# Pacing one stream of weight loads through a feed-forward stage, splitting GpSimd's subtractions, and leaving out eight dot products

## The chip, the cores and the metric

The kernel runs on one core of one Trainium2 chip. The metric is the time of one execution on the device, in microseconds (us). Five engines take part, each with its own queue of instructions that it works off in order: TensorE (PE in the profile; its weight loads are PEld), VectorE (DVE), ScalarE (ACT), GpSimd (POOL) and SyncE (SP), which here issues the transfers from and to the main memory (DMAs).

## The reference

The reference runs two blocks over a sequence of 512 tokens of width 1024. Cut to what matters:

```python
def first_block(x, ...):
    x = x + 0.5 * swiglu(rms_norm(x, ffn1_norm), ffn1_w_in, ffn1_w_out)   # the first FFN, D_FF = 2816
    ...                                # RWKV-7 time mixing, dilated attention, gates, w_out
    x = x + 0.5 * swiglu(rms_norm(x, ffn2_norm), ffn2_w_in, ffn2_w_out)   # the second FFN

def hybrid_layer(x, ctx, c, c_ctx, row, col, last, ...):                  # twice
    shift, scale, gate = split(silu(c) @ w_mod + b_mod, 3)                # the modulation
    shift_c, scale_c, gate_c = split(silu(c_ctx) @ w_mod + b_mod, 3)
    h  = rms_norm(x, norm_w) * (1 + scale) + shift
    hc = rms_norm(ctx, norm_w) * (1 + scale_c) + shift_c
    ...                                # latent attention, grouped attention, convolution
    x_new = x + gate * (y @ w_out)
    if last:
        return x_new, ctx
    ctx_new = ctx + gate_c * (yc @ w_out)
    return x_new, ctx_new
```

All values are 32-bit floats. The modulation is, for each of the two layers, 24 groups of 128 outputs (8 of shift, 8 of scale, 8 of gate), each for two vectors of length 1024: c and c_ctx. In the last layer gate_c is computed from its definition but used by nobody, since ctx is returned as it is.

## The kernel before

**Products in three parts.** Each weight chunk comes from the main memory as a tile wraw of 128 x up to 1024 floats (wload, L570, 512 KB for 1024 columns, two buffers). ScalarE rounds it into whi, the form that TensorE takes (L583), and the rest, wraw - whi, goes into wlo (L585 to L587). The argument on says who subtracts: 0 is GpSimd in one instruction, a number above 0 is VectorE in so many instructions. whi and wlo have three buffers each. The inputs stand in pairs in the same way (HH and HL, FH and FL), and each product is three matmuls: whi by high, whi by low, wlo by high (mm3, L617). A chunk of 1024 columns is eight slices of 128 columns, and so 24 matmuls of 128x128 by 128x512; wlo is first read by the third. wfill (L591) keeps one chunk split and one more loaded ahead of the chunk in use.

**The first FFN** (ffn_steps and ffn_stream, L701 to L813) has 44 chunks of w1 (22 pairs: gate, pg, and up, pu) and 24 of w2 (po), in the order 16 of w1, 8 of w2, 14, 8, 14, 8: 68 chunks in all, those of w2 with 8, 7 and 7 slices. After each pair of w1 chunks the gating runs (act, L731): on VectorE fa = pg x rs, then after ScalarE's tanh fa = (fs + 1) x fa, fb = pu x rs, fb = fb x fa, then after ScalarE's rounding FH, FL = fb - FH. Two of these five read the accumulators (PSUM) and rs; three have both operands in SBUF. Four accumulators (ffmm) are free for pg, pu and po. All of these chunks are split with on = 0, by GpSimd. The low-rank projections (pl, lora_steps) follow the FFN.

**The modulation** (mod_steps, L1531) is computed during the first FFN: 48 tiles wm of 128 x 1024 floats are loaded through SP (L1544, two buffers), and for each VectorE makes two dot products with the broadcast vectors (L1547, scalar_tensor_tensor with an accumulated sum, into the throw-away tile mjunk), one for c and one for c_ctx. The results M are next read in the second FFN.

**What sets the order.** The kernel's steps are generators. drive (L438) runs them twice: first it records an order by its own clock of the engines (Clock, L192, with costs such as 130 + 2.13 n ns for a GpSimd instruction with n columns), taking the step that could start first; a step's priority is added to that time, and mod_steps has 2000 ns. A step may wait for a flag (flags, need, count, L421 and L650 to L666). The second run replays the order. Below it a scheduler orders the instructions of each engine by a priority that counts up with each instruction; FF1_LATE (L21) puts mod_steps 500 back. Each engine then works off its queue in that order, and waits for semaphores only at its head.

Line 318, which every row of the profile names, is the helper through which all instructions go; rows are told apart by tile.

Of the kernel before, what the change touches and what calls it, by code (L numbers as in the profile page):

```python
# [17 lines left out]
RW_PRIO = {"stream": 2000, "fill": 5000}  # L18
RW_LATE = {"rw_stream": 500, "rw_fill": 500, "qkv_chain": -1000}
RW_AHEAD = 3000  # L20
FF1_LATE = {"norm": -500, "stats": -300, "mod_steps": 500}  # L21
FF2_PRIO = 300
X_LATE = {"proj_steps": 1000, "taps": 1000, "out_steps": 300}
# [168 lines left out]
class Clock:  # L192
    def __init__(self):
        self.t = {e: 0.0 for e in ("PE", "DVE", "ACT", "POOL", "SP")}
        self.gaps = {e: [] for e in self.t}
        self.room = GAPS[0]
        self.dma = 0.0
        self.acc = {}
        self.floor = {}
        self.slots = {}  # L200
        self.act_set = None
        self.last = 0.0
        self.free_run = False
# [324 lines left out]
class K:  # L528
    def __init__(self, tc, A, ctx, plan):
        self.clk = Clock()  # L530
        self.plan = plan
        self.flags = Flags(self.clk)
        self.A = A
        self.tc = _TC(tc, self.clk)
        self.nc = nc = _NC(tc.nc, self.clk)
        tc = self.tc
        E = ctx.enter_context
        self.const = E(tc.tile_pool(name="const", bufs=1))
        self.xp = E(tc.tile_pool(name="xp", bufs=1))
        self.hp = E(tc.tile_pool(name="hp", bufs=1))  # L540
        self.wp = E(tc.tile_pool(name="wp", bufs=3))
        self.sm = E(tc.tile_pool(name="sm", bufs=2))
        self.wraw, self.wq, self.wi = [], [], 0
        self.held = False
        self.fine = 4
        self.late = {}
        self.tk, self.nb = {}, {}
        npar = A["par"].shape[1]
        self.onescol = self.const.tile([P, 1], F32, name="onescol")
        nc.vector.memset(self.onescol, 1.0)  # L550

        warm = self.sm.tile([P, 1], F32, name="warm", bufs=1)
        nc.scalar.activation(warm, self.onescol, AF.Silu)
        self.wfill(0, 1)
        self.par_t = self.cload("par", [P, npar])
        self.acc = self.const.tile([P, T], F32, name="acc")
        self.M = [self.const.tile([P, 24, 2], F32, name=f"mod{l}") for l in range(2)]
# [12 lines left out]
    def wload(self, name, idx, a, b):  # L570
        raw = self.wp.tile([P, 1024], F32, tag="wraw", name="wraw", bufs=2)
        src = self.A[name]
        for i in idx:
            src = src[i] if not isinstance(i, tuple) else src[:, i[0]:i[1]]
        self.nc.sync.dma_start(raw[:, :a * b].rearrange("p (a b) -> p a b", a=a), src)
        return raw, a, b

    def wsplit(self, raw, a, b, on):
        nc = self.nc
        n = a * b  # L580
        hi = self.wp.tile([P, 1024], F32R, tag="whi", name="whi", bufs=3)
        lo = self.wp.tile([P, 1024], F32R, tag="wlo", name="wlo", bufs=3)
        nc.scalar.copy(hi[:, :n], raw[:, :n])  # L583

        for i in range(max(on, 1)):  # L585
            s = slice(i * n // max(on, 1), (i + 1) * n // max(on, 1))
            (nc.vector if on else nc.gpsimd).tensor_sub(lo[:, s], raw[:, s], hi[:, s].bitcast(F32))  # L587
        v = lambda t: t[:, :n].rearrange("p (a b) -> p a b", a=a)
        return v(hi), v(lo)
# [624 lines left out]
    def rw_tile(self, H, w, fin=None, chain=None):  # L1214
# [5 lines left out]
        for x in range(8):  # L1220

            ahead = RW_AHEAD if x % 4 else 0
            self.tc._tc.cur_priority -= ahead
# [307 lines left out]
    def mod_steps(self, stack):  # L1531

        nc = self.nc
        mp = stack.enter_context(self.tc.tile_pool(name="modp", bufs=1))
        cc = mp.tile([P, 2, 1024], F32, name="cc")
        junk = mp.tile([P, 1024], F32, name="mjunk")
        yield "Fffn1_normrs", 1, "ACT"
        nc.sync.dma_start(cc, self.A["cc"])
        nc.scalar.activation(cc, cc, AF.Silu)
        for l in range(2):  # L1540
            M = self.M[l]
            for m in range(24):
                w = mp.tile([P, 1024], F32, tag="wm", name="wm", bufs=2)
                nc.sync.dma_start(w, self.A[f"l_mod_{l}"][m])  # L1544
                for s in range(2):
                    yield "DVE"
                    nc.vector.scalar_tensor_tensor(junk, w, 1.0, cc[:, s], ALU.mult, ALU.mult, accum_out=M[:, m, s:s + 1])  # L1547
            yield "DVE"
            o, n = PAR_COLS[f"b_mod_{l}"]
            nc.vector.tensor_add(M, M, self.par_t[:, o:o + 24].unsqueeze(2).to_broadcast([P, 24, 2]))  # L1550
            o, n = PAR_COLS[f"norm_w_{l}"]
            nc.vector.tensor_scalar_add(M[:, 8:16], M[:, 8:16], 1.0)
            nc.vector.tensor_mul(M[:, 8:16], M[:, 8:16], self.par_t[:, o:o + 8].unsqueeze(2).to_broadcast([P, 8, 2]))

            nc.vector.tensor_scalar_mul(M[:, 16:24], M[:, 16:24], 0.5)
# [875 lines left out]
def body(tc, A, out, plan):  # L2431
    with ExitStack() as ctx:
# [9 lines left out]
        with ExitStack() as lor:  # L2442
            k.lora_setup(lor)
            k.late = FF1_LATE
            with ExitStack() as c2:
# [51 lines left out]
```

## Time and profile before

| | us |
|---|---|
| median of three runs | 2564.78 |
| lowest and highest of the three | 2545.41 and 2572.88 |
| the profiled execution | 2555.58 |
| its span, first to last instruction | 2553.8 |

The mean granted TensorE clock of the profiled execution is 0.948 of full speed. The page of the profile gives the busy time of each engine and the chain of work that ended last, followed back from the last instruction; further views are the table of busy times by stage, the timeline of an engine, the waits and the groups of equal instructions. A row of a timeline has the start, the duration, the engine, the operation and the tiles (out<-in); what stands in brackets is the idle time before it and what ended that.

### The profile page before, as it was taken

How to read it: one execution, taken by the hardware profiler on the slowest of the kernel's cores; microseconds unless marked ns; L12 is line 12 of the kernel's file. 1: busy time of each engine (PE TensorE's matmuls, PEld its weight loads, DVE VectorE, ACT ScalarE, POOL GpSimd, SP SyncE). 2: the span in 40 equal slices, each digit the busy share in tenths (PEclk: the TensorE clock that was granted, in tenths of full speed). 3: DMA queues.
4: the chain of work that ended last, by engine and by line, in shares of the span. 5: the costliest groups of instructions: out<-in, count | busy, mean ns of one | idle time of the engine just before them, and what ended most of it. 6: DMA issues, size and time to landing. Idle time of an engine off the chain costs nothing.

```text
span 2553.8 us, 33817 instructions
## 1 busy us (share of the span) xinstructions
PE 2372.9 (93%) x12556; PEld 1920.0 (75%) x12556; DVE 1703.2 (67%) x3157; ACT 1014.7 (40%) x1852; POOL 745.1 (29%) x441
## 2 busy tenths in 40 slices
PE   8798999999999999989989899999889999789897
PEld 6576887877777777757878788888677778677776
DVE  8999357676666656534767846664559865568865
ACT  4212224334233333335433533333335655345553
POOL 4444443010111110212423233335332332232331
PEclk9998999999889869979999999999899999899998
DMA  6555323433223224332423232433310222310221
GB/s 210 188 199 180 100 95 107 121 86 102 79 56 105 66 56 117 130 121 79 127 96 113 82 128 74 145 109 112 128 61 25 71 63 67 116 47 26 64 78 53
DMA packets 122196, 254.24 MB, mean 100 GB/s; under 512 B 39208, under 2 KB 54576, under 8 KB 121392
## 3 DMA queue, kind: packets, MB, share of 16 engines
q1 hardware_dynamic: 122032, 252.09, 31.6%
q8 instruction: 99, 1.62, 0.3%
q14 instruction: 65, 0.53, 0.1%
HBM read 222.07 MB, written 21.59 MB: 95 GB/s over the span
## 4 chain that ended last, share of the span: by engine, by line
PE 68%; DVE 19%; ACT 4%; issue 4%; DMA 2%; POOL 2%; SPq 0%; DVEq 0%; ACTq 0%; POOLq 0%
PE prj L318 12%; PE po L318 11%; PE pj L318 7%; PE pu L318 6%; PE pg L318 6%; DVE mjunk L318 5%; PE pm L318 4%; PE pwo L318 4%; PE sc L318 3%; PE pt L318 2%; DVE c0cy L318 1%; DVE fb L318 1%; PE pA L318 1%; DMA wm<-in_l_mod 1%; PE pl L318 1%
## 5 line engine op out<-in xcount | busy, mean ns | idle before, releaser
L318 POOL TENSOR_TENSOR wlo<-wraw,whi 128x1024 fp32r<-128x1024 f32 (+5 forms) x239 | 552.3, 2312 | 1012.6 <-ACT whi L318 926.4
L318 ACT CAST whi<-wraw 128x1024 fp32r<-128x1024 f32 (+4 forms) x330 | 324.8, 984 | 584.3 <-PE po L318 110.7
L318 PE MATMUL prj<-HH,whi 128*128 128x512 f32 x464 | 197.4, 426 | 0.0
L318 PE MATMUL prj<-HH,wlo 128*128 128x512 f32 x464 | 190.9, 412 | 0.0
L318 PE MATMUL prj<-HL,whi 128*128 128x512 f32 x464 | 187.4, 404 | 0.0
L318 DVE SCALAR_TENSOR_TENSOR mjunk<-wm,cc 128x1024 f32<-128x1024 f32 x96 | 165.5, 1724 | 6.1 <-DMA wm<-in_l_mod 4.7
L318 PE MATMUL po<-FH,whi 128*128 128x512 f32 x352 | 141.1, 401 | 13.2 <-ACT FH L318 13.1
L318 DVE TENSOR_TENSOR wlo<-wraw,whi 128x512 fp32r<-128x512 f32 (+1 forms) x149 | 122.5, 832 | 41.6 <-ACT whi L318 35.8
L318 PE MATMUL pu<-HH,wlo 128*128 128x512 f32 x352 | 139.0, 401 | 11.9 <-POOL wlo L318 11.9
L318 PE MATMUL pg<-HH,whi 128*128 128x512 f32 x352 | 139.5, 396 | 8.2 <-ACT HH L318 7.3
L318 PE MATMUL pu<-HH,whi 128*128 128x512 f32 x352 | 141.4, 402 | 1.3 <-ACT whi L318 1.3
L318 PE MATMUL po<-FL,whi 128*128 128x512 f32 x352 | 140.2, 398 | 0.8 <-DVE FL L318 0.8
L318 PE MATMUL po<-FH,wlo 128*128 128x512 f32 x352 | 139.8, 397 | 1.1 <-POOL wlo L318 1.1
L318 PE MATMUL pu<-HL,whi 128*128 128x512 f32 x352 | 140.2, 398 | 0.0
L318 PE MATMUL pg<-HL,whi 128*128 128x512 f32 x352 | 139.0, 395 | 0.5 <-DVE HL L318 0.5
L318 PE MATMUL pg<-HH,wlo 128*128 128x512 f32 x352 | 135.8, 392 | 1.1 <-POOL wlo L318 1.1
L318 DVE TENSOR_TENSOR ptl<-pt,pth 128x512 fp32r<-128x512 f32 x156 | 105.1, 685 | 36.3 <-ACT pth L318 35.3
L318 PE MATMUL pj<-HH,whi 128*128 128x512 f32 (+1 forms) x304 | 123.2, 409 | 3.2 <-ACT HH L318 3.2
L318 POOL TENSOR_TENSOR se<-SV,EC 64x128 f32<-64x128 f32 x56 | 36.3, 648 | 302.4 <-DVE SV L318 238.8
L318 PE MATMUL pj<-HL,whi 128*128 128x512 f32 (+1 forms) x304 | 123.4, 407 | 0.6 <-DVE HL L318 0.6
L318 PE MATMUL pj<-HH,wlo 128*128 128x512 f32 (+1 forms) x304 | 123.7, 408 | 0.0
L318 ACT ACTIVATE pr<-sc,am 128x768 f32<-128x768 f32 (+1 forms) x120 | 98.0, 818 | 58.7 <-DVE am L318 54.4
(745 smaller groups left out, 5974.2 us busy)
## 6 DMA issues: line engine op xcount, KB each, us to landing
wraw<-in_ffn_w SPq DMA_DIRECT2D x96, 512.0 KB, 3.3
wm<-in_l_mod SPq DMA_DIRECT2D x48, 512.0 KB, 3.5
wraw<-in_l_b SPq DMA_DIRECT2D x45, 512.0 KB, 3.4
wraw<-in_w_rkv SPq DMA_DIRECT2D x24, 512.0 KB, 3.7
wraw<-in_w_qkv SPq DMA_DIRECT2D x18, 512.0 KB, 3.3
wraw<-in_w_gate SPq DMA_DIRECT2D x16, 512.0 KB, 3.9
wraw<-in_ffn_w SPq DMA_DIRECT2D x16, 448.0 KB, 3.4
xd<-X SPq DMA_DIRECT2D x24, 256.0 KB, 3.0
```

What stands on the lines that cost most here:

```text
L318: r = real(*a, **kw)
```

## The change

Three things. First, each modulation load has a place: load i (0 to 47) may be recorded only when weight load k = 6 + 60 i / 48 (rounded down) has been recorded, and on SP's queue it stands behind that weight load (issue_after). So the 48 loads are tied to chunks 6 to 64 of the 68. Second, GpSimd's subtraction of a chunk with n columns comes as n // 256 instructions of equal width (four for 1024, three for 896 and 768, two for 640) instead of one. Third, for the last eight tiles of the second layer's modulation (its gate) only the dot product with c is made; the column for c_ctx, which nobody reads, is set to zero once.

```diff
+MOD_FROM, MOD_OVER = 6, 60
@@ wload
-        self.nc.sync.dma_start(raw[:, :a * b].rearrange("p (a b) -> p a b", a=a), src)
+        self.wdma.append(self.nc.sync.dma_start(raw[:, :a * b].rearrange("p (a b) -> p a b", a=a), src).ins)
+        self.count("wdma")
@@ wsplit
-        for i in range(max(on, 1)):
-            s = slice(i * n // max(on, 1), (i + 1) * n // max(on, 1))
+        parts = on or n // 256
+        for i in range(parts):
+            s = slice(i * n // parts, (i + 1) * n // parts)
             (nc.vector if on else nc.gpsimd).tensor_sub(lo[:, s], raw[:, s], hi[:, s].bitcast(F32))
@@ mod_steps
+        nc.vector.memset(self.M[1][:, 16:24, 1], 0.0)
         for l in range(2):
             M = self.M[l]
             for m in range(24):
+                k = MOD_FROM + (24 * l + m) * MOD_OVER // 48
+                yield "wdma", k + 1, "DVE"
                 w = mp.tile([P, 1024], F32, tag="wm", name="wm", bufs=2)
-                nc.sync.dma_start(w, self.A[f"l_mod_{l}"][m])
-                for s in range(2):
+                with self.tc.issue_after(self.wdma[k]):
+                    nc.sync.dma_start(w, self.A[f"l_mod_{l}"][m])
+                for s in range(1 if l == 1 and m >= 16 else 2):
                     yield "DVE"
                     nc.vector.scalar_tensor_tensor(junk, w, 1.0, cc[:, s], ALU.mult, ALU.mult, accum_out=M[:, m, s:s + 1])
```

## Rows read from the trace of the kernel before

**Rows 1.** The page: busy time of each engine, and the chain that ended last.

```profile
PE 2372.9 (93%) x12556; PEld 1920.0 (75%) x12556; DVE 1703.2 (67%) x3157; ACT 1014.7 (40%) x1852; POOL 745.1 (29%) x441
PE 68%; DVE 19%; ACT 4%; issue 4%; DMA 2%; POOL 2%; SPq 0%; DVEq 0%; ACTq 0%; POOLq 0%
```

**Rows 2.** By stage: stretch and length, busy (count) by engine, clock, DMA share, GB/s.

```profile
61.00:132.00 71.00, 52.04 (x216) 40.66 (x214) 70.48 (x84) 14.96 (x20) 33.93 (x10) 0.91 0.55 182
...
185.00:256.00 71.00, 62.37 (x244) 49.40 (x243) 68.56 (x86) 14.56 (x19) 29.61 (x10) 0.90 0.55 182
...
307.00:382.00 75.00, 75.00 (x332) 62.10 (x332) 42.30 (x33) 21.31 (x27) 35.08 (x14) 1.00 0.29 94
```

**Rows 3.** The chain from 0 to 450 us: its shares, then start, duration, what.

```profile
by line: DVE mjunk L318 27.0%; PE po L318 16.5%; PE pg L318 10.5%; PE pu L318 9.4%; issue 7.0%; DMA wm<-in_l_mod 5.9%; DVE fb L318 4.7%; DVE fa L318 4.3%; PE pl L318 3.9%; DVE FL L318 2.0%; PE prj L318 1.7%; DMA X<-in_xT 1.1%; DVE mod L318 
...
29.26 4.82 PE pg L318 x14
...
271.26 35.03 PE po L318 x149
...
311.75 5.44 PE pu L318 x24
...
421.52 2.32 PE pl L318 x10
```

**Rows 4.** Timeline of VectorE and of GpSimd, 60 to 77 us.

```profile
61.22 1.22 DVE L318 SCALAR_TENSOR_TENSOR mjunk<-wm,cc 128x1024 f32<-128x1024 f32 x1
...
62.48 3.29 DVE L318 SCALAR_TENSOR_TENSOR mjunk<-wm,cc 128x1024 f32<-128x1024 f32 x1
...
76.87 3.27 DVE L318 SCALAR_TENSOR_TENSOR mjunk<-wm,cc 128x1024 f32<-128x1024 f32 x1
...
61.24 3.44 POOL L318 TENSOR_TENSOR wlo<-wraw,whi 128x1024 fp32r<-128x1024 f32 x1 [5.97 <-ACT whi L318]
```

**Rows 5.** Waits (total, times, longest): SP 61 to 132, TensorE 0 to 440.

```profile
SPq L318 <- DVE mjunk L318: 52.1, 15, 4.7
...
PE po L318 <- ACT FH L318: 12.4, 1, 12.4
PE pu L318 <- POOL wlo L318: 11.9, 7, 2.5
```

**Rows 6.** GpSimd's subtractions by width: busy us, mean ns, idle before and releaser.

```profile
L318 POOL TENSOR_TENSOR wlo<-wraw,whi 128x1024 fp32r<-128x1024 f32 x156 | 402.7, 2583 | 702.6 <-ACT whi L318 623.0 <-PE pm L318 39.8 <-PE pt L318 13.6
...
L318 POOL TENSOR_TENSOR wlo<-wraw,whi 128x896 fp32r<-128x896 f32 x26 | 56.6, 2176 | 103.2 <-ACT whi L318 101.1 <-PE pt L318 2.1
...
L318 POOL TENSOR_TENSOR wlo<-wraw,whi 128x256 fp32r<-128x256 f32 x7 | 5.2, 741 | 28.8 <-ACT whi L318 24.3 <-PE po L318 4.5
```

**Rows 7.** VectorE's groups in the second FFN, 1320 to 1820 us, columns as above.

```profile
L318 DVE TENSOR_TENSOR fb<-fb,fa 128x512 f32<-128x512 f32 x22 | 31.4, 1426 | 0.6
...
L318 DVE TENSOR_TENSOR FL<-fb,FH 128x512 fp32r<-128x512 f32 x22 | 22.6, 1025 | 6.9 <-ACT FH L318 6.9
...
L318 DVE TENSOR_TENSOR fa<-pg,rs 128x512 f32<-128x512 f32 x22 | 15.2, 690 | 35.1 <-PE pg L318 35.1
```

**Rows 8.** Timeline of VectorE and GpSimd around 560 us and around 1403 us.

```profile
559.84 2.69 DVE L318 TENSOR_TENSOR wlo<-wraw,whi 128x512 fp32r<-128x512 f32 x2 [0.19 <-ACT whi L318]
560.10 1.28 POOL L318 TENSOR_TENSOR AR<-r,Ee 128x512 f32<-128x512 f32 x1
...
1402.54 1.89 DVE L318 SCALAR_TENSOR_TENSOR c0glu<-cg,c0glu 128x256 f32<-128x256 f32 x1 [1.17 <-ACT cg L318]
1404.11 1.04 POOL L318 TENSOR_TENSOR ul<-uw,uh 128x320 fp32r<-128x320 f32 x1
```

**Rows 9.** The chain between 1180 and 2060 us: start, duration, what.

```profile
1368.72 2.81 DVE fb L318
...
1813.08 2.41 POOL wlo L318
...
1906.78 2.77 DVE x0cy L318
```

More of the change, by code (lines that the diff above doesn't have):

```diff
@@ L542, in __init__ @@
         self.sm = E(tc.tile_pool(name="sm", bufs=2))
-        self.wraw, self.wq, self.wi = [], [], 0
+        self.wraw, self.wq, self.wi, self.wdma = [], [], 0, []
         self.held = False
```

## The prediction, made before the result

> **What bounds the kernel now.** I read the page first. TensorE is busy for 93% of the span, but only 68% of the chain that ended last is TensorE and 19% is VectorE [rows 1]. So there is time in which TensorE waits for VectorE, and the next question is where. The table by stage answers it: in the first FFN TensorE makes 332 matmuls in the 75 us from 307 on, but only 216 in the 71 us from 61 on and 244 in those from 185 on, and in those two stretches VectorE is busy for 70.48 and 68.56 of the 71 us [rows 2]. The chain of the first 450 us names the work: 27.0% of it is the modulation's dot products (mjunk), which end at 271 us on the chain; from there on it is TensorE, one weight chunk of 24 matmuls every 5.44 us [rows 3].
>
> The price of this. At 29.26 us the chain has TensorE at the second pair of chunks, 66 of the FFN's 68 chunks ahead of it; the LoRA projection (pl) starts at 421.52 [rows 3]. Undisturbed, 42 chunks of w1 and 8 of w2 in the first part cost 50 x 5.44 = 272.0 us, and the other 16 of w2, with 21 matmuls of 5.44/24 = 0.227 us, cost 16 x 4.76 = 76.2 us: 348.2 us, and TensorE took 421.5 - 29.3 = 392.3. **The first FFN gives away 44.1 us.** No change of its pace can return more than this.
>
> How it is lost is in two views. In the timeline GpSimd subtracts from 61.24 to 64.68 us, and a dot product that VectorE starts at 62.48 ends at 65.77, 1.1 us behind it: it ran when GpSimd had finished, taking 3.29 us in place of 1.22. The pattern comes back at 76.87, 14.39 us later, for two chunks that cost TensorE 10.88 when nothing disturbs it [rows 3, 4]. So a GpSimd subtraction and a VectorE instruction with two operands in SBUF take turns, and before, three loads' dot products (six) fell on each pair of chunks. In the waits, SP stands 52.1 us of 71 with a modulation load for which VectorE has to give a buffer back; the next weight load is behind it in the queue. Then TensorE waits for wlo up to 2.5 us at a time (11.9 us in seven waits), and once 12.4 us for FH, whose chain stands behind dot products [rows 5].
>
> **Part 1, pacing.** Load i now waits for the recording of weight load 6 + 1.25 i and is queued behind it: 48 loads over chunks 6 to 64, 1.6 loads for a pair of chunks in place of 3. The DMAs are the same 48, on the same queue, each behind a weight load instead of ahead of it where VectorE was fastest. VectorE's own work for a pair of w1 chunks is then 3.2 x 1.22 = 3.9 us and five instructions of the gating at about 0.69 [rows 4, 7], together 7.4 of 10.88 us. The turns with GpSimd: three of the five gating instructions have two SBUF operands, 3.9 + 3 x 0.69 = 6.0; GpSimd's two subtractions, whole, 2 x 2.4 = 4.8 (2.41 undisturbed [rows 9]; the mean with waits is 2.58 [rows 6]). That is 10.8 of 10.88 us: just enough, where before it was 6 x 1.22 + 2.1 + 4.8 = 14.2 for a period of 14.39. In the w2 stretches nothing of the gating runs, and 1.6 x 1.22 + 2.4 = 4.4 of 5.44 us a chunk leaves room. So nearly all of the 44 us can come back, but with no margin in w1.
>
> Behind a waiting modulation load stands the next weight load, and behind that ACT's whi, GpSimd's wlo and TensorE. The load needs the dots of two loads before, 2.5 chunks (13 us) old when it is issued; I cost this at nothing as long as VectorE keeps up, and as rival D if not.
>
> **Part 2, subtractions in parts.** Each of the 156 subtractions of 1024 columns becomes four of 256, each of the 26 of 896 three. A 256-column one has a mean of 741 ns: 4 x 0.741 = 2.96 against 2.58 (with waits) or 2.4, so 0.4 to 0.6 us more GpSimd time for each, at most 239 x 0.56 = 134 us on an engine with 745.1 of 2553.8 us busy [rows 1, 6]. It lies beside TensorE except where wlo is on the chain. What it gives: TensorE's third matmul of a chunk needs only the first part, 1.7 us earlier, about the size of the seven waits; and a VectorE instruction waits for a part (up to 0.74 us), not for up to 2.4. In turns, though, a pair of chunks now asks 6.0 + 2 x 2.4 to 2 x 2.96, 10.8 to 11.9 us of 10.88. With 19 pairs of w1 chunks under modulation, that is 0 to 19 x 1.0 = 19 us; the smaller figure is nearer, since part of a record may be GpSimd's own start, which it can do while VectorE has its turn (the record from 61.24 is 3.44 us long, 1.0 more than undisturbed, and a dot product of 1.22 us that VectorE began at 61.22 lies in it [rows 4, 9]). I take 0.5 us a pair: 9.5 us. To this come three borders from w1 to w2, where FH and FL of the last tile may find a dot and a part ahead of them, 1.5 us each: 4.5. **Excess after: 14 us; bounds 5 and 32** (every part met by VectorE: 2 x 2.96 + 7.4 = 13.3 a pair, 2.4 x 19 = 46, less what w2 stretches take up, about a third). Gain of the first FFN: 44.1 - 14 = **30 us, from 12 to 39**.
>
> Whether VectorE gets its turn between two parts is the open point. Two places of this kernel show two GpSimd records in a row with a VectorE instruction waiting, and they differ. At 559.84 two half-subtractions of VectorE take 2.69 us and end at 562.53; they ran only when AR, which GpSimd began at 560.10 right behind another one, was through at 561.38. At 1402.54 c0glu ends at 1404.43, 0.3 us after GpSimd's next record (ul) began at 1404.11: there VectorE went between [rows 8]. I weigh the second higher, because it is between 128-partition subtractions as here. [...]
>
> **Part 2 in the rest.** In the second FFN fb and FL have means of 1426 and 1025 ns where an instruction that reads PSUM, and never waits for GpSimd, has 690: (0.74 + 0.34) x 22 = 24 us of waiting [rows 7]. What counts is the chain: ten such rows stand on it from 1368.72 (fb, 2.81) to 1906.78 (x0cy, 2.77) with 1.2 to 2.1 us of waiting each, about 16 us; where GpSimd itself is on the chain (1813.08, wlo 2.41) the parts cost 0.5 us each [rows 9]. A part instead of the whole takes away about 10 of the 16, of which I keep half, since the next releaser is often close, with 2 for the second layer and 2 less for wlo: **gain 5 us, from -15 to +15**; the lower end is a changed order of work, for the planner's GpSimd clock and the scheduler's priority count move with every added instruction.
>
> **Part 3, eight dot products less.** They stand in the last eight loads, chunks 56 to 64, where the squares and the U splits of the last w2 part also want VectorE. 8 x 1.22 = 10 us of VectorE, included above through 88 instead of 96; alone, where TensorE leads, nothing.
>
> **Sum.** 2555.58 us (the profiled execution; span 2553.8) - 30 - 5 = **2521 us**. The median of the runs is 2564.78, 9 us higher, and their spread is 27 us; I leave the forecast at the sum.
>
> **Rivals.**
> A, as above: 2521, own range 2500 to 2538. Chance 0.48.
> B, the parts hang together: pacing still works, but a pair of w1 chunks asks 6.0 + 2 x 2.96 = 11.9 us, 1.0 more than TensorE, so the excess is 19 + 4.5 = 23 and the gain 21; the ten waits on the chain grow by 0.56 each: 2555.6 - 21 + 6 = 2541. For it: the rows at 560. Against it: those at 1404. 0.18.
> C, TensorE leads everywhere in the first FFN (excess 5) and the chain's waits go wholly: 2555.6 - 39 - 16 = 2500. For it: the stretch from 307 on, where a 2.4 us wait of VectorE costs TensorE nothing. 0.14.
> E, the FFN gain is used up later: of the 134 us that GpSimd's parts cost at most, a fifth comes onto the chain, where wlo and VectorE's waits for GpSimd already stand: 2555.6 - 30 + 27 = 2553. For it: the wlo row of the chain. Against it: GpSimd is busy 29% of the span. 0.12.
> D, the other side: the modulation load's wait on SP. If VectorE falls behind by over 13 us, every one of the 48 loads stands before the buffer is free, and each holds the weight load behind it. Before, that wait was 3.5 us each [rows 5]. It decides from 0.9 us of TensorE loss a load (48 x 0.9 = 44 us); at 1.5 us it is 72 - 44 = 28 more: 2584. For it: in w1 the turns leave no margin. Against it: w2 stretches let VectorE catch up. 0.08.
>
> **How the numbers follow.** Predicted: A, 2521. Faster by over 1% (below 2539; about what a measurement of this kernel can tell): A 0.46, C 0.14, half of B, 0.09, together 0.69. Within 1%: the rest of B and A and most of E, 0.21. Slower: D and a tail of E, 0.10. The range takes in C and B, and E by half: 2492 to 2556.
>
> **What would show it.** In the profile after: pl starts at 380 to 395 us in place of 421.5; no dot product over 2 us, its mean below 1.5; the chain of the first 400 us mostly TensorE; about 1.6 modulation loads for a pair of chunks, the last at about 370 us; SP's waits for mjunk near none; fb and FL of the second FFN below 1.0 us. If fb and FL stay at 1.4 or rise, B holds. If SP still waits for mjunk and TensorE for wlo, D. If the FFN is shorter and the total isn't, E. Wrong altogether would be a first FFN that stays near 392 us with VectorE idle: then dot products were not what held it.

## The result, and the profile after

The kernel after takes 2522.45 us (median of four runs, 2510.65 to 2525.89); the kernel before, beside it on the same chip, 2568.83 (2545.41 to 2574.96). The ratio is 0.9853, with a 95% interval of 0.9805 to 0.9902. Measured again later with more runs, after took 2527.74 us against 2552.94: 0.9906, interval 0.9872 to 0.9940. The profiled execution of after took 2522.58 us (span 2520.8) against 2555.58 before, 33 us less. The forecast was 2521 us.

To see where the 33 us lie, I cut both traces at the same instructions: the first matmul of pl, the last start of prj (the end of the RWKV mixing's projections), the first and last of the merge's pm, the first pj behind it, the last pg, the last pwo. Lengths in us, worked out from the times that the views by tile give:

| stretch | before | after | difference |
|---|---|---|---|
| first FFN, to pl | 421.4 | 388.6 | -32.8 |
| RWKV mixing | 657.5 | 652.7 | -4.8 |
| end of the mixing and attention | 133.5 | 146.8 | +13.3 |
| merge | 79.5 | 79.6 | +0.1 |
| to the first pj | 22.4 | 20.9 | -1.5 |
| second FFN | 469.5 | 464.4 | -5.1 |
| two layers and end | 770.0 | 767.8 | -2.2 |

So the first FFN gave the whole gain, and the rest came out even: small gains here and there, and one loss of 13 us that nothing in the prediction speaks of. Each column is one execution. Two profiles of one and the same kernel (after, and further down the one with parts in the second FFN alone) differ by 4.1 and 2.9 us in the first FFN and by 1.0 and 8.9 in the mixing, so the small differences of this table are not shown by it alone.

The page after: busy time of each engine, GpSimd's subtractions, the dot products, and the modulation loads (last number: median us from issue to landing).

```profile
PE 2377.5 (94%) x12556; PEld 1924.6 (76%) x12556; DVE 1564.7 (62%) x3142; ACT 1015.8 (40%) x1852; POOL 923.9 (37%) x1039
...
L320 POOL TENSOR_TENSOR wlo<-wraw,whi 128x256 fp32r<-128x256 f32 (+3 forms) x837 | 734.2, 906 | 827.8 <-ACT whi L320 731.5
...
L320 DVE SCALAR_TENSOR_TENSOR mjunk<-wm,cc 128x1024 f32<-128x1024 f32 x88 | 123.3, 1401 | 82.1 <-DMA wm<-in_l_mod 81.6
...
wm<-in_l_mod SPq DMA_DIRECT2D x48, 512.0 KB, 4.5
```

Against [rows 1], VectorE is busy 138.5 us less and GpSimd 178.8 us more. A dot product now takes 1.40 us on the mean. The chain that ended last is followed back over the last 3% of the span only in this profile, so it can't be read for the first FFN; the table by stage and the waits stand in for it.

The table by stage, over the stretches of [rows 2] (stretch and length, busy and count by engine, granted clock, DMA share, GB/s):

```profile
61.00:132.00 71.00, 67.54 (x284) 54.73 (x283) 46.65 (x65) 17.45 (x20) 47.12 (x47) 0.95 0.49 163
185.00:256.00 71.00, 68.34 (x287) 55.54 (x286) 52.15 (x73) 16.99 (x21) 48.43 (x45) 0.95 0.47 160
307.00:382.00 75.00, 74.11 (x324) 60.50 (x323) 44.94 (x62) 26.55 (x35) 46.13 (x51) 1.00 0.52 175
```

Where TensorE made 216 and 244 matmuls in 71 us, it makes 284 and 287, and VectorE, full before, is busy 66 to 73% of these stretches. The dot products now reach into the third stretch, which was free of them.

The waits of the first 400 us (total, times, longest), of SP, VectorE and TensorE:

```profile
SPq L320 <- DVE mjunk L320: 1.0, 1, 1.0
```

```profile
DVE mjunk L320 <- DMA wm<-in_l_mod: 81.6, 41, 5.1
```

```profile
PE pg L320 <- ACT HH L320: 6.4, 1, 6.4
PE po L320 <- DVE FL L320: 5.2, 3, 2.7
PE po L320 <- ACT FH L320: 1.8, 1, 1.8
```

SP's wait for a dot product to give a buffer back, 52.1 us of 71 in [rows 5], is gone. TensorE's waits for wlo (11.9 us) and the one of 12.4 for FH are gone too. In their place VectorE waits for wm: the load comes after VectorE is ready for it.

Two things beside these waits belong to the 32.8 us. TensorE comes to the same matmul of the second pair 2.9 us earlier, at 26.12 us in place of 29.02, ahead of all dot products, since it waits less for rmsr there. The timelines, before and after:

```profile
28.61 0.65 PE L318 MATMUL rb<-c_ident,rmsr 128*128 128x128 f32 x4 [3.04 <-DVE rmsr L318]
29.02 0.47 PE L318 MATMUL pg<-HL,whi 128*128 128x512 f32 x1
```

```profile
25.71 0.65 PE L320 MATMUL rb<-c_ident,rmsr 128*128 128x128 f32 x4 [0.84 <-DVE rmsr L320]
26.12 0.48 PE L320 MATMUL pg<-HL,whi 128*128 128x512 f32 x1
```

And TensorE's clock: from this matmul to pl it stands still for 28.2 us before and 7.0 after, and it starts 55 matmuls before and 26 after while its granted clock is 0.50 of full speed. Those come every 0.427 us in place of 0.227, which makes about 11 us before and 5 after. The waits were the larger part of the loss, not all of it.

The timeline of VectorE and of GpSimd answers the open point of the prediction:

```profile
66.15 1.28 DVE L320 SCALAR_TENSOR_TENSOR mjunk<-wm,cc 128x1024 f32<-128x1024 f32 x1 [1.19 <-DMA wm<-in_l_mod]
...
74.49 1.76 DVE L320 SCALAR_TENSOR_TENSOR mjunk<-wm,cc 128x1024 f32<-128x1024 f32 x1
```

```profile
63.29 4.75 POOL L320 TENSOR_TENSOR wlo<-wraw,whi 128x256 fp32r<-128x256 f32 x4 [2.13 <-ACT whi L320]
...
74.17 4.08 POOL L320 TENSOR_TENSOR wlo<-wraw,whi 128x256 fp32r<-128x256 f32 x4 [1.31 <-ACT whi L320]
...
85.16 2.83 POOL L320 TENSOR_TENSOR wlo<-wraw,whi 128x256 fp32r<-128x256 f32 x4 [1.09 <-ACT whi L320]
```

Four parts with no dot and no fb or FL beside them (the four from 85.16 on) take 2.83 us, 0.71 each. The four from 63.29 on last to 68.04, 4.75 us, because VectorE goes in between: the dot from 66.15 ends at 67.43, inside them. And VectorE's own instructions are late by about half a microsecond (the dot from 74.49 takes 1.76 in place of 1.22 and ends at 76.25, inside the four from 74.17 to 78.25), not by the 2.07 us of [rows 4], where a whole subtraction stood ahead. VectorE does get its turn between two parts.

The gating's rows in the second FFN, to set against [rows 7] (columns as there):

```profile
L320 DVE TENSOR_TENSOR FL<-fb,FH 128x512 fp32r<-128x512 f32 x22 | 21.2, 963 | 6.9 <-ACT FH L320 6.9
L320 DVE TENSOR_TENSOR fb<-fb,fa 128x512 f32<-128x512 f32 x22 | 19.7, 895 | 0.6
```

### The profile page after: what moved, and what is told of

Same layout as the page of the kernel before. It is cut to its first block, busy times and chain, and to the rows that moved or that the text cites. A ratio compares the mean times of both kernels' runs of the same rounds, so it can differ in the third digit from the quotient of the medians.

```text
span 2520.8 us, 34512 instructions
## 1 busy us (share of the span) xinstructions
PE 2377.5 (94%) x12556; PEld 1924.6 (76%) x12556; DVE 1564.7 (62%) x3142; ACT 1015.8 (40%) x1852; POOL 923.9 (37%) x1039
## 5 line engine op out<-in xcount | busy, mean ns | idle before, releaser
L320 POOL TENSOR_TENSOR wlo<-wraw,whi 128x256 fp32r<-128x256 f32 (+3 forms) x837 | 734.2, 906 | 827.8 <-ACT whi L320 731.5
L320 DVE SCALAR_TENSOR_TENSOR mjunk<-wm,cc 128x1024 f32<-128x1024 f32 x88 | 123.3, 1401 | 82.1 <-DMA wm<-in_l_mod 81.6
```

Of the source, the lines that this page charges most:

```text
L320: r = real(*a, **kw)
```

## Experiments

All ratios are against the kernel before, measured beside it on the same chip, with the 95% interval. "pl" is the start of the first matmul of pl. In the diffs, "-" is the kernel after.

**Taking the parts of the change apart.** First, after without the pacing:

```diff
-                k = MOD_FROM + (24 * l + m) * MOD_OVER // 48
-                yield "wdma", k + 1, "DVE"
                 w = mp.tile([P, 1024], F32, tag="wm", name="wm", bufs=2)
-                with self.tc.issue_after(self.wdma[k]):
-                    nc.sync.dma_start(w, self.A[f"l_mod_{l}"][m])
+                nc.sync.dma_start(w, self.A[f"l_mod_{l}"][m])
```

> The changed kernel without the pacing: the modulation loads go again as early as SP takes them; subtractions in parts and 88 dot products stay. Theory (pacing and parts each carry a share of the first FFN): three loads fall again on a pair of w1 chunks, SP waits again for dot products (over 60 us up to 300 us, against 1 us with pacing), the low-rank projection pl starts at 402 to 418 us against 388 with pacing and 421 before. Total 2535 to 2552. Rival (the parts alone do it, because TensorE then waits only for the first part of wlo): pl at 388 to 395 and a total within 8 us of the changed kernel.

Measured: 2541.05 us, ratio 0.9954 (0.9932 to 0.9977); pl at 399.6, between what the theory (402 to 418) and the rival (388 to 395) gave; the total is the theory's. Then after with whole subtractions:

```diff
-        parts = on or n // 256
+        parts = max(on, 1)
```

> The changed kernel with GpSimd's subtractions whole again; pacing and 88 dot products stay. Theory: pl starts at 394 to 404 us (a pair of w1 chunks has room, but a VectorE instruction waits up to 2.4 us and FH and FL are later at the borders), fb and FL of the second FFN have means of 1.4 and 1.0 us again, and the stages behind the first FFN give back some 13 us apart from the clock of the mixer's end. Total 2530 to 2545. Rival (pacing alone does it): pl at 387 to 391 and a total within 5 us of the changed kernel.

Measured: 2520.39 us, ratio 0.9882 (0.9837 to 0.9927); pl at 385.5, earlier than in after. The total is within 2.1 us of after's: the rival holds, pacing alone does it. The first start of pl in the view by tile, without the pacing and without the parts:

```profile
L320 PE MATMUL pl<-UH,whi x24: 387/395/404, 399.6 to 417.1; 128*128 128x512 f32 x16, 128*32 128x512 f32 x8
```

```profile
L320 PE MATMUL pl<-UH,whi x24: 388/392/404, 385.5 to 403.0; 128*128 128x512 f32 x16, 128*32 128x512 f32 x8
```

So the two parts don't add up. From 421.4, the pacing alone takes off 36 us and the parts alone 22 (the eight dot products are left out in both); together they take off 33. Either one loosens the same knot, VectorE's dots behind whole subtractions, and once the pacing has done so the parts cost a little. What the kernel without the pacing has left is in its waits of the first 400 us, of TensorE and of SP:

```profile
PE po L320 <- ACT FH L320: 11.3, 1, 11.3
```

```profile
SPq L320 <- DVE mjunk L320: 83.0, 38, 4.6
```

The long wait for FH at the first border from w1 to w2 is still there (12.4 us in [rows 5]). It stands behind dot products: VectorE makes five of them, 7.9 us, between FL of the tile before at 110.63 us and fb at 120.79. Only the pacing removes it.

Then all 96 dot products (the line with range(1 if ... else 2) back to range(2), and the memset taken out):

> The changed kernel with all 96 dot products (the eight for c_ctx in the last layer's gate are made and their column isn't set to zero). Theory: they cost 10 us of VectorE in the last w2 part, where VectorE has room: pl at 388 to 391, total within 5 us of the changed kernel. Rival (the tail of the first FFN has no room on VectorE): pl 8 to 10 us later.

Measured: 2526.65 us, ratio 0.9896 (0.9861 to 0.9930); pl at 391.2. The ratio lies between the two of after, 0.9853 and 0.9906. The eight dots are worth nothing that shows in the time; pl is 1.7 us later than in the latest of the five profiles of kernels with parts there and 88 dots (384.5 to 389.5), which one profile can't settle.

**Is it the rate, or the place in SP's queue?** The pacing does two things: it spreads the loads, and it puts each behind a weight load. This kernel keeps the second and goes back to three loads for a pair of chunks:

```diff
-MOD_FROM, MOD_OVER = 6, 60
+MOD_FROM, MOD_OVER = 6, 32
```

> As the kernel after, but the 48 loads are tied to chunks 6 to 38 instead of 6 to 64: three loads for a pair of chunks, as before, still each queued behind its weight load. Theory 1 (the rate of dot products for a pair of chunks decides): six dots and the gating ask more than a pair's 10.9 us, pl starts at 397 to 405 us, near the kernel with parts and without pacing (399.6), and TensorE waits for FL, FH or wlo again. Theory 2 (the place on SP's queue behind the weight load decides): pl stays at 387 to 391 us.

Measured: 2537.34 us, ratio 0.9942 (0.9912 to 0.9972); pl at 401.0, where the kernel without any pacing had 399.6. Its waits, of TensorE and of SP:

```profile
PE po L320 <- ACT FH L320: 13.9, 3, 10.2
```

```profile
SPq L320 <- DVE mjunk L320: 70.0, 33, 3.6
```

The waits are back as well. The rate is what counts, as theory 1 had it; at three loads a pair the place in the queue gives nothing. That the 48 loads slow down the weight loads themselves is not what happens: the FFNs' weight loads of 1024 columns land 3.3 us after their issue (median) in before and in this kernel, and 3.4 in after.

**Does VectorE's new wait for wm cost anything?** Each load is recorded before the dots of the load before it (the two dots of a load are made when the next load has been recorded):

```diff
...
+                if prev is not None:
+                    yield from dots(*prev)
+                prev = w, l, m
...
```

> As the kernel after, but each modulation load is recorded before the dot products of the load before it, so it is asked for one load earlier in VectorE's order. Theory 1 (VectorE's new waits of 81.6 us for wm push the gating behind them): these waits fall below 30 us and pl starts 2 to 5 us earlier, at 383 to 387 us. Theory 2 (TensorE leads, and VectorE's waiting lies beside it): the waits go or move, pl stays at 387 to 390 us, and the time is that of the kernel after within 3 us.

Measured: 2524.86 us, ratio 0.9909 (0.9870 to 0.9948); pl at 389.5.

```profile
DVE mjunk L320 <- DMA wm<-in_l_mod: 84.8, 42, 5.1
```

The waits didn't move, 84.8 against 81.6 us, so the edit missed its lever: the load stands behind its weight load on SP wherever it is recorded. Time and pl are those of after, as theory 2 had it, but this run doesn't show that the waits are free. That most of them are is argued from TensorE's waits above, only 7.0 us behind VectorE's and ScalarE's FL and FH in the whole first FFN; at the borders they do cost something, as the rows below show.

**Where the parts pay.** Parts only for the chunks of the first FFN, and only for those of the second (the chunk's name is handed to wsplit):

```diff
-        parts = on or n // 256
+        parts = on or (n // 256 if name.startswith("ffn1") else 1)
```

> Parts of 256 columns only for the chunks of the first FFN, whole subtractions in all other stages; pacing and 88 dot products stay. Theory: pl at 388 as in the changed kernel; in the stages behind it the waits of VectorE come back (fb and FL of the second FFN 1.4 and 1.0 us), which costs 8 to 15 us in the stretches where TensorE's clock is the same in both. Total 2525 to 2540. Rival (the parts are worth nothing behind the first FFN): the stages behind pl take the same time, total within 5 us of the changed kernel, whichever way the clock falls.

Measured: 2519.86 us, ratio 0.9889 (0.9850 to 0.9929); pl at 387.9. The total is within 2.6 us of after's, as the rival had it, but not because the parts do nothing behind pl: the second FFN takes 468.3 us, 3.9 more than in after, and the stretch behind the mixing 132.9, 13.9 less. With "ffn2" in place of "ffn1":

> As the kernel after (pacing, 88 dot products), but GpSimd subtracts in parts of 256 only for the chunks of the second FFN, and whole everywhere else. My theory (what the parts give lies in the second FFN; what they cost lies at the end of the RWKV mixing, where TensorE's granted clock falls): pl starts at 384 to 388 us as with whole subtractions, the stretch behind the mixing takes 133 to 137 us with no fall of the clock, the second FFN 464 to 466 us instead of 469.6; in all some 5 us below the kernel with whole subtractions and 5 to 10 below the kernel after. Rival (the second FFN's gain came from a changed order of earlier work): the second FFN stays at 468 to 470 us, and the time equals that with whole subtractions.

Measured: 2502.31 us, ratio 0.9800 (0.9733 to 0.9867); pl at 382.9, the second FFN 465.2 us, the stretch behind the mixing 125.9. The rival falls: the second FFN is shortened by its own parts, not by an earlier order. The longest of the gating's waits, fb in the second FFN, in this kernel and in the one with whole subtractions:

```profile
L320 DVE TENSOR_TENSOR fb<-fb,fa 128x512 f32<-128x512 f32 x22 | 20.0, 909 | 0.6
```

```profile
L320 DVE TENSOR_TENSOR fb<-fb,fa 128x512 f32<-128x512 f32 x22 | 29.1, 1322 | 0.6
```

The first FFN is the other way about. With the pacing, pl starts at 382.9 to 385.8 in the five profiles with whole subtractions there, and at 384.5 to 389.5 in the five with parts and 88 dots: 2.7 us later on the mean. Two things are in this. The parts bring TensorE to the matmul of 26.12 us above 2.5 us earlier (26.1 to 26.9 us in place of 28.6 to 29.1), and from there to pl it takes 5.2 us longer (358.4 to 363.2 in place of 354.0 to 357.1). The timeline of VectorE in after, at the first and the second border, and TensorE's of both show where this is lost:

```profile
107.26 1.22 DVE L320 SCALAR_TENSOR_TENSOR mjunk<-wm,cc 128x1024 f32<-128x1024 f32 x1 [1.01 <-DMA wm<-in_l_mod]
...
108.41 0.69 DVE L320 TENSOR_TENSOR FL<-fb,FH 128x512 fp32r<-128x512 f32 x1
...
232.72 1.23 DVE L320 SCALAR_TENSOR_TENSOR mjunk<-wm,cc 128x1024 f32<-128x1024 f32 x1 [2.60 <-DMA wm<-in_l_mod]
```

```profile
109.16 0.80 PE L320 MATMUL po<-FL,whi 128*128 128x512 f32 x1 [1.69 <-DVE FL L320]
...
234.62 0.79 PE L320 MATMUL po<-FL,whi 128*128 128x512 f32 x1 [2.66 <-DVE FL L320]
```

```profile
110.00:114.00 4.00, 4.00 (x10) 3.06 (x10) 0.94 (x3) 1.04 (x1) 2.76 (x4) 0.50 0.00 0
...
234.00:238.00 4.00, 3.38 (x8) 2.71 (x9) 3.80 (x7) 0.94 (x1) 1.41 (x1) 0.50 0.41 166
```

FL stands behind a dot for whose load VectorE has just waited, 1.01 and 2.60 us; TensorE stands 1.69 and 2.66 us, and at each of these places its granted clock falls to 0.50 of full speed, by this row and its neighbours for about 7 us each. In the kernel with whole subtractions the waits for FL here are 0.6 us each, with one for FH of 1.58, and the clock falls less: at the second border 0.83 and 0.74 in two rows of 4 us, at the first not at all. Over the five profiles of either kind TensorE stands 4.0 us longer with parts (7.1 in place of 3.1 us from that matmul to pl), which is most of the 5.2. The fall doesn't always follow: in the kernel with whole subtractions for w_pr (below) TensorE stands 2.85 us at the second border and the clock stays at 1.00.

```profile
234.91 0.50 PE L320 MATMUL po<-FL,whi 128*128 128x512 f32 x1 [2.85 <-DVE FL L320]
```

```profile
234.00:238.00 4.00, 3.09 (x13) 2.56 (x14) 3.93 (x7) 0.95 (x1) 1.40 (x2) 1.00 0.52 208
```

**The 13 us behind the mixing.** In after, TensorE's clock falls to 0.50 where the last serial chain of the mixing begins, and its steps take 5.9 us each in place of 3.4. Two theories: the parts of the eight w_pr chunks, which are split just there, or the order of the work before. First these eight whole (w_gate is VectorE's in any case):

```diff
-        parts = on or n // 256
+        parts = on or (n // 256 if name not in ("w_gate", "w_pr") else 1)
```

> As the kernel after, but the chunks used behind the RWKV mixing (w_gate, which VectorE splits anyway, and w_pr) are subtracted whole; parts everywhere else. Theory 1 (these chunks' parts stand around the last serial chain of the mixing and delay or reorder it until TensorE's granted clock falls): the clock stays at 1.00 to the end of the mixing, the stretch behind it takes 133 to 137 us instead of 146.8, the time is 10 to 13 us below the kernel after. Theory 2 (the fall comes from how the work before it is ordered, with parts anywhere outside the first FFN): the clock falls as in the kernel after, 145 to 149 us, same time as after.

Measured: the clock stays at 1.00, the stretch takes 126.2 us. The time is 2517.55 us, ratio 0.9869 (0.9786 to 0.9952), with the four runs spread from 2495 to 2532: the stretch is as theory 1 has it and shorter, the gain of 10 to 13 us isn't to be seen in the totals. Then the other way, these eight chunks alone in parts and nothing else (name == "w_pr"):

> The kernel with pacing and whole subtractions, but the eight chunks of w_pr behind the RWKV mixing in parts of 256, and nothing else. Theory 1 (these eight chunks' parts by themselves let the granted clock fall): 0.50 from the end of the mixing on, the stretch behind it takes 143 to 149 us, some 10 to 13 us above the kernel with whole subtractions, at 2525 to 2540 us. Theory 2 (the fall needs parts in the mixing ahead of it too): the clock stays at 1.00 through the last serial chain, 125 to 137 us, and 2510 to 2525 us.

Measured: the clock falls, 149.9 us; 2532.86 us, ratio 0.9910 (0.9873 to 0.9947). And after once more, to see whether the fall belongs to the kernel:

> The kernel after again, beside the other three on one chip, as their yardstick and for a second profile of it. If the fall of TensorE's granted clock at the end of the RWKV mixing belongs to its order of work, it is there again, the stretch behind the mixing takes 143 to 149 us, and the time is 2515 to 2528 us. If it was an accident of one execution, the stretch takes 125 to 137 us in this one.

Measured: 2527.74 us, ratio 0.9906 (0.9872 to 0.9940); it falls again, 147.8 us. Theory 1 holds from both sides. Over all profiles the clock falls there in the seven with parts for w_pr (143.7 to 149.9 us) and in none of the seven without (125.9 to 136.6; there it falls only behind the chain). The table by stage of the kernel with only these eight in parts, and of the one with whole subtractions (the clock is the third number from the end):

```profile
1046.00:1050.00 4.00, 1.19 (x9) 0.80 (x9) 1.44 (x3) 1.57 (x4) 3.69 (x5) 1.00 1.00 323
1050.00:1054.00 4.00, 4.00 (x20) 2.91 (x18) 0.28 (x1) 0.65 (x3) 0.39 (x1) 0.59 0.94 319
1054.00:1058.00 4.00, 4.00 (x17) 2.92 (x17) 0.28 (x1) 0.39 (x2) 0.39 (x1) 0.50 0.19 72
```

```profile
1043.00:1047.00 4.00, 2.13 (x17) 1.49 (x16) 2.35 (x4) 2.34 (x5) 3.94 (x2) 1.00 1.01 336
1047.00:1051.00 4.00, 4.00 (x28) 2.87 (x28) 0.70 (x3) 1.04 (x4) 0.65 (x2) 1.00 0.85 280
1051.00:1055.00 4.00, 4.00 (x29) 2.94 (x28) 0.28 (x1) 0.78 (x3) 0.53 (x2) 1.00 0.28 108
```

And how it comes about, in the two timelines. With the eight in parts:

```profile
1039.51 3.44 POOL L320 TENSOR_TENSOR wlo<-wraw,whi 128x256 fp32r<-128x256 f32 x4 [5.18 <-ACT whi L320]
...
1042.97 0.33 SPq L320 DMA_DIRECT2D wraw<-in_w_pr  x1
...
1043.36 1.17 SPq L320 DMA_DIRECT2D gtd<-gt  x1
...
1048.52 0.69 ACT L320 ACTIVATE gt<-prj,bgh 128x512 f32<-128x512 f32 x1 [1.75 <-DMA gtd<-gt]
...
1049.25 0.50 PE L320 MATMUL pm<-HH,whi 128*128 128x512 f32 x1 [2.00 <-ACT gt L320]
```

With whole subtractions:

```profile
1037.28 2.41 POOL L320 TENSOR_TENSOR wlo<-wraw,whi 128x1024 fp32r<-128x1024 f32 x1 [5.79 <-ACT whi L320]
...
1039.71 0.33 SPq L320 DMA_DIRECT2D wraw<-in_w_pr  x1
...
1040.10 0.42 SPq L320 DMA_DIRECT2D gtd<-gt  x1
...
1045.31 0.69 ACT L320 ACTIVATE gt<-prj,bgh 128x512 f32<-128x512 f32 x1 [0.77 <-DMA gtd<-gt]
...
1046.05 0.50 PE L320 MATMUL pm<-HH,whi 128*128 128x512 f32 x1 [1.02 <-ACT gt L320]
```

The parts take 3.44 us in place of 2.41. They hold the buffer wraw a microsecond longer, the next weight load on SP goes out 3.46 us after the subtraction began in place of 2.43, the transfer of gt stands behind that load on SP, gt waits for the transfer (its buffer is read by it), and TensorE waits for gt: 2.00 us in place of 1.02, and the clock falls. That is argued from these two timelines, and what exactly decides stays open. With the fall, this last gap is 0.95 to 2.02 us over the seven profiles; without it, 0.34 to 1.12. The two overlap, so the length of this gap alone isn't it.

**The version that puts this together**: whole subtractions in the first FFN and for w_pr, parts everywhere else.

```diff
-        parts = on or n // 256
+        parts = on or (1 if name[:4] == "ffn1" or name in ("w_gate", "w_pr") else n // 256)
```

> Pacing, 88 dot products, and parts of 256 everywhere except in the first FFN, where they cost some 3 us, and for the chunks of w_pr, where they cost some 12. Theory 1 (parts in the mixing and the two layers give something too): the mixing takes 650 to 654 us instead of 657 to 664, and the time is 2488 to 2498 us, below the kernel with parts in the second FFN alone. Theory 2 (all the gain is in the second FFN): 2498 to 2508 us, the same as that kernel, with first FFN 383 to 386 us and second FFN 463 to 466 us.

Measured: 2515.03 us, ratio 0.9877 (0.9828 to 0.9927). Its stretches are about as theory 2 has them (first FFN 385.5 us, second 462.6; mixing 661.4, not the 650 to 654 of theory 1), and the time is above both theories. Beside it once more the kernel with parts in the second FFN alone:

> The kernel with pacing and parts in the second FFN alone, again, to compare with after and with the kernel with parts nearly everywhere on one chip: 2495 to 2508 us, 0.5 to 1.2% below the kernel after, no fall of the clock at the end of the mixing. If its lead of the last call was the chance of four executions, it comes out at 2510 to 2520 us, like the kernel with whole subtractions.

Measured: 2510.74 us, ratio 0.9859 (0.9806 to 0.9912): 0.7% below after on the same chip, as forecast, but in time just inside the range that was to speak for chance. So its lead over the kernel with whole subtractions (0.9882) isn't settled by the totals; what the profiles bear out is the second FFN: with parts there it takes 462.6 to 467.9 us, without them 468.2 to 469.6, about 4 us apart on the mean. Of the ten runs of this kernel seven are below the fastest of the fifteen of after (2510.65); the medians are 2508.2 and 2523.2, 15 us or 0.6% apart, but over several chips, on which the kernel before itself has medians from 2546.77 to 2568.83. On the one chip that had both, the medians are 17 us apart and the two intervals overlap. It is probably faster than after, and clearly faster than before. Parts in the mixing and the layers add nothing that these runs show.

## Why the prediction was right, point by point

**The time.** 2521 forecast, 2522.58 in the profiled execution against which the sum was made. The first FFN, 30 of the 35 us, came as forecast. The rest did not: +5 forecast, 0.2 measured. That the sum came out within 2 us is in part luck: a loss of 13.3 us that it didn't contain is balanced by gains elsewhere, 4.8 of them in the mixing, where two profiles of one kernel differ by 8.9.

**The first FFN.** A gain of 30 us forecast, 32.8 measured; pl at 388.6, within 380 to 395. From the same matmul on it is 421.4 - 29.0 = 392.4 before and 388.6 - 26.1 = 362.5 after, 29.9 less, and 362.5 - 348.2 = 14.3 of excess, where the sum had 14; the second profile of after gives 384.5 - 26.1 - 348.2 = 10.2. The other 2.9 us lie ahead of that matmul, where the sum had nothing. One count in it is off: at 29.26 the chain's row has only 14 of its chunk's 24 matmuls left, so 348.2 is 2.3 us too much, and both losses are 2.3 us larger than written, 46.4 before and 16.6 after. The make-up of the excess was wrong. The turns of dots and parts, sized at 9.5 us, have at most some 4 us left for them, and VectorE had idle time (81.6 us of waiting for wm) where the sum saw none. The borders, sized at 1.5 us each, cost 7.0 us of waits and with them some 5 us of matmuls at half clock. The sum had put a dot and a part ahead of FL; what the rows show there is VectorE waiting for the dot's load. The other signs were as named: no dot over 2 us (the longest is 1.85), a mean of 1.40, the last load at 353.7 us (370 forecast), 1.0 us of SP waiting for mjunk.

**The parts in the first FFN.** The prediction gave the pacing nearly all of the 44 us and the parts a price of 0 to 19, taken at 9.5, and 4.5 for the borders. The runs show 36 for the pacing alone, and for the parts 5.2 us less 2.5 at the head, a price of 2.7. That the parts take off 22 us by themselves, where nothing is paced, stands in no step of it.

**Rival B**, that the parts hang together, is refuted by the timeline above, where a dot ends inside four parts. The row of before at 1402.54 was the right one of the two in [rows 8]. fb and FL fell to 895 and 963 ns, from 1426 and 1025 in [rows 7].

**Rival D**, that the modulation load holds up SP, is refuted: 1.0 us. **Rival C** came true in part: TensorE leads nearly everywhere in the first FFN, but the waits of the rest were not returned as a whole. **Rival E**, the gain used up later by GpSimd's longer time, is right in its kind and wrong in its place and size: wlo's parts cost 13 us at the end of the mixing, where TensorE's clock falls, and not as a fifth of GpSimd's longer time (it grew by 178.8 us, beyond the 134 allowed for, since a part's record also holds its wait for VectorE: a part of 256 columns in the first FFN has a mean of 1.01 us, 0.71 in the four from 85.16 on). That it comes by SP's queue, held up by 1.0 us, is argued from the one pair of timelines.

**The rest.** +5 us forecast, 0.2 measured. The gain was sized about right: "a part instead of the whole takes away about 10 of the 16, of which I keep half", and the second FFN with the stretch behind the merge gave 6.6 us. The term that failed is the price beside it, "2 less for wlo": the parts of the eight w_pr chunks cost 13.3 us. It counted only what waits for wlo. The longer time of the parts (3.44 us in place of 2.41 in the pair of timelines) also delays what waits for the end of wlo's reading: the buffer wraw, and so the transfers behind the next weight load on SP, which went out 3.46 us after the subtraction began in place of 2.43; and no term held a fall of TensorE's clock, to 0.50 here.

**The eight dot products.** Nothing forecast, nothing seen.

## What to carry to other kernels

Two edits against the same wait didn't add up here: 36 us and 22 alone, 33 together. Try each alone before shipping both, for the second may then only bring its price. When an instruction is split to let another engine in, count what the longer total (here 3.44 us in place of 2.41) delays, the buffers it reads and the queue behind their next load among it, and split only where another engine's wait for it holds up the one that bounds the kernel. And look at TensorE's clock along a long serial chain: where it fell to 0.50 at the chain's start, here behind a gap of 0.95 to 2.02 us, the stretch took 143.7 to 149.9 us in place of 125.9 to 136.6.

## What the runs showed of the hardware

- Four 256-column subtractions of GpSimd took 2.83 us with no dot and no fb or FL of VectorE beside them, one of 1024 columns 2.41. Beside VectorE's dots and gating, or its HL at the end of the mixing, the four took 3.44 to 4.75 in the rows shown, and a dot of VectorE ended inside them.
- TensorE's clock fell to 0.50 in the middle of the kernel when it had stood still 0.95 to 2.66 us, in the mixing with another gap of 0.85 us shortly before; with gaps of up to 1.12 us there, and of 2.85 us in the first FFN, it stayed at 1.00 in other kernels. In the mixing it then stayed low through the whole serial chain, whose steps took 5.86 us in place of 3.35, though the view shows TensorE busy almost all the time.
- Runs of one and the same kernel spread over 15 to 38 us along with the mean granted clock: the kernel with parts in the second FFN took 2489.10 us at 0.960 and 2526.85, on another chip, at 0.946. Differences under 10 us are read from the stretches, not from the totals.
- A modulation load landed 4.5 us after its issue (median) in the kernel after, against 4.1 without the pacing and 3.5 before. What lengthens it, the place behind a weight load or something else, is not shown.
